# Four PSUM banks in turn, sampled columns on GpSimd, sampled values' products by fours, and other places for the chunks

## The chip, the cores and the metric

The kernel runs on one core of a Trainium2 chip. The metric is the device time of one execution in microseconds; for the kernel before it is the median of three runs. An engine has its own queue of instructions and works it in order: TensorE (PE; its weight loads are PEld), VectorE (DVE), ScalarE (ACT), GpSimd (POOL) and SyncE (SP, which here only issues transfers). Engines wait for each other on semaphores.

## The reference

One decoder step with two mixer branches on the same normalised input: 512 prompt positions and 8 sampled tokens (one each, with states of their own), so 520 columns are carried through all projections.

```python
h = _rmsnorm(x, norm_g)
P = hf @ w_in                                  # one projection for both branches
q, k, v, g_a, sh, g_b, m_a, m_b = split(P)
y_a, s_ret_new = _retention_branch(q, k, v, g_a, pos0, s_ret)      # 4 heads, DK 256, DV 512
y_b, s_rw_new = _rwkv_branch(sh, sh_prev, g_b, ..., s_rw)          # 16 heads of 64
merged = sigmoid(m_a) * (y_a @ w_down_a) + sigmoid(m_b) * (y_b @ w_down_b)
x = x + merged @ w_out
gate = sigmoid(_rmsnorm(x, ple_norm_g) @ w_ple_gate)
x = x + (p @ w_ple) * gate
```

The retention branch is attention with a decay and a state; the RWKV branch is a recurrence `s = s * w - (s kk) (a kk) + v k`, which the kernel solves for the prompt in chunks of 64 positions, two heads at a time. Outputs are the final norm of `x` for prompt and sampled tokens, and all new states.

## The kernel before

**Precision and projections.** Everything is float32. A weight tile `raw` (512 KB) is loaded by SyncE (`fetch`, L136), copied by ScalarE to a rounded `whi` (L141), and VectorE takes the rest as `wlo` (L142). A projection is then three products (`hhi` x `whi`, `hlo` x `whi`, `hhi` x `wlo`, line L154) that accumulate in one PSUM bank, 24 matmuls for one half of the 520 columns. They are the bulk of TensorE's work.

**PSUM.** There are eight banks: pool `ph` has four, for projections (`mm_half`); pool `px` has three, handed out by `bank()`; pool `pq` has one, tag `po`. A bank can be written again when its last reader is done with it.

**Who sets the order.** The functions emit instructions through a scheduler that runs a simulated timeline and places each instruction on its engine's queue by priority and readiness; dependences added by hand (`side_by_side`: order only; `after`: a semaphore) restrict it. Which buffer of a pool a tile gets is settled in the order of the code. So the order on the chip is fixed at build time, and each engine then takes its queue strictly in order.

**Stages in the trace.** To 82 us: input norm, transposes, key projections and the norm sums `pss` (L410). 82 to 262 us: eight RWKV pairs (`pair`, two heads each). 262 to 715 us: four retention heads. 715 to 867 us: the eight RWKV chunks between gate and down projections. To the end: the rest of the down projections, the output projection and the per-layer gates.

**A pair** makes, in this order: two `pn` (L438, norms; read by VectorE into `kkn`), four `pw` (L445 and L446, two products each; read by ScalarE's tanh at L447 into `sg` and `a`), decays and the scaled keys `KRS`, `BK` on VectorE (`km`, L471, on the way); then 16 small products `g` into four banks (L498), which VectorE masks into `GM` (L504); two `pb` (L483, the bonus `bon`); transposes of `BK` (L525) and of the values (L532). `bank()` serves all of these from `px`, but for the fourth bank of `g`, which is `pq`'s. Between the parts stand the next pair's projections `zr`, `zv` (or gates `mg`) as filler. Stores of `KRS`, `GM`, `BKT`, `Vt`, `bon` go to DRAM on SyncE. ScalarE also copies the eight sampled columns of five tensors into `smp` (L488, 40 small copies in all); at the end of the pairs `smp` is transposed (L579), evicted to `sT` (L580) and stored to `SMd` (L581). GpSimd reads `SMd` back as `sv` (L659), prepares constants, and then loads the retention states `tS` (L749), which ScalarE scales (L755).

**A retention head** projects and rotates keys and queries (L792, L801 to L806), then values: `phv` (L827) takes the four weight tiles j = 0 to 3, 24 matmuls each. The sampled tokens' values are made apart, in `vsm` (L822): for j = 1 and 3 four products, each a float32 matmul with 32 columns of the array, one for each of four column groups; a float32 matmul shows as two passes in the trace. `side_by_side` keeps the four in order but lets the scheduler put other work among them, or the next four right behind. In the built program `vsm` stands in groups of 6 and 2 (head 0), 5 and 3 (heads 1 and 3), 5, 2 and 1 (head 2).

**A chunk** (`chunk`) has products `UO` (L1014), `U` (L1023), `dS` (L1029), `UO` again (L1032), with evictions between (`Ot`, L1045). Between the chunks stand 16 fills, eight gates `mg` (L208, stored to `MBd`, L209) and eight down projections `down_a`; the list `AT` says how many fills are emitted up to each chunk. Chunks have a high priority, so the scheduler moves them ahead of fills when they are ready. `loads(c)` (L990 to L999) brings a chunk's `SV`, `KR`, `TT`, `BKt`, `DT`.

Of the kernel before, what the change touches and what calls it, by code (L numbers as in the profile page):

```python
# [8 lines left out]
F32 = mybir.dt.float32  # L9
# [3 lines left out]
ALU = mybir.AluOpType  # L13
# [66 lines left out]
def body(tc, A, O, dbg=None, upto="Z"):  # L80
# [11 lines left out]
    with es:  # L92
# [12 lines left out]
        def ctile(name, shape):  # L105
            return cst.tile(shape, F32, tag=name, name=name)

        def bank(name="x", tag="x"):
            return px.tile([128, 512], F32, tag=tag, name=name)

# [71 lines left out]
        def side_by_side(ms):  # L182

            ms = [getattr(i, "ins", i) for i in ms]
            for x, y in zip(ms, ms[1:]):
                tc.add_manual_dep(y, x.name, mybir.DependencyInfo(mybir.DependencyClass.NoSync, mybir.DependencyReason.SCHED_ONLY),
                                  reason="side by side")

        def after(i, prior):

            tc.add_manual_dep(getattr(i, "ins", i), getattr(prior, "ins", prior).name,
                              mybir.DependencyInfo(mybir.DependencyClass.Sync, mybir.DependencyReason.DATA), reason="together")
# [189 lines left out]
        for p in range(NPAIR):  # L382
# [25 lines left out]
            for j, c0, c1 in HV:  # L408
                for x, w in enumerate(sqs):
                    pe.matmul(pss[j][0:16, 0:c1 - c0], indr[:, p, :], w[:, c0:c1], start=(p == 0 and x == 0), stop=(p == 7 and x == 1))  # L410
        rn2 = pA.tile([32, NT], F32, tag="b1", name="rn")
        rn = rn2[0:16]
# [20 lines left out]
        def pair(p, zr, zv):  # L433
# [44 lines left out]
            def bonus():  # L478
                bon = pA.tile([128, NT], F32, tag="bon", name="bon")
                for j, c0, c1 in HV:  # L480
                    pb = bank("pb")[:, 0:c1 - c0]
                    for x, w in enumerate(rks):
                        pe.matmul(pb, bdr, w[:, c0:c1], start=(x == 0), stop=(x == 1))  # L483
                    dve.tensor_tensor(bon[:, c0:c1], pb, zv[:, c0:c1], ALU.mult)
                act.activation(bon, bon, AF.Identity, bias=vcol(V_LB, p))
                sp.dma_start(BNd[p], bon)
                for i, src, f in ((0, zr, 1.0), (2, km, 1.0), (3, zv, 1.0), (4, kkn, 1.0), (5, b1, 0.5)):
                    act.activation(smp[:, p, i, :], src[:, T:NT], AF.Copy, scale=f)  # L488

            if p == NPAIR - 1:  # L490
# [5 lines left out]
                   else pA.tile([128, NCH, 128], F32, tag=f"W{i}", name="GM", bufs=1) for i in range(2)]  # L496
            gs = [bank("g") for _ in range(3)] + [pq.tile([128, 512], F32, tag="po", name="g")]
            ms = [pe.matmul(gs[2 * q + hh][:, c * 128:(c + 1) * 128], BK[hs_, 4 * q + c, :], KRS[hs_, 4 * q + c, :], start=True, stop=True)  # L498
# [77 lines left out]
        for q in range(2):  # L576
# [3 lines left out]
            act.activation(sT[:, q * 512:(q + 1) * 512], g[0:48], AF.Copy)  # L580
        sp.dma_start(SMd.rearrange("v b d -> (v b) d"), sT)  # L581
        pA_.__exit__(None, None, None)
        for nm, t in dict(KRd=KRd, BKd=BKd, DTd=DTd, XTd=XTd, Vd=Vd, BNd=BNd, SMd=SMd).items():
# [200 lines left out]
        for h in range(H):  # L784
# [33 lines left out]
            for j in range(4):  # L818
                ready = fetch(w_in[256 * j:256 * j + 256, O_V + DV * h:O_V + DV * h + DV])
                raws, w = raws[-1:] + [wide(ready[0])], [wide(t) for t in weights(None, ready=ready)]  # L820
                if j % 2:
                    side_by_side([pe.matmul(vsm[32 * g:32 * g + 32], hst[:, 2 * j - 2 + g, :], raws[g // 2][:, g % 2, :],  # L822
                                            start=(j == 1), stop=(j == 3), skip_group_check=True) for g in range(4)])
                for jt in range(4):
# [263 lines left out]
        nxt_y = beside_rwkv(128, slice(0, 128))  # L1088
        AT = [0, 2, 4, 6, 8, 9, 11, 13, 16]
        for c in range(NCH):  # L1090
# [228 lines left out]
```

## Time and profile before

| what | value |
|---|---|
| time, median of 3 runs | 1083.75 us (1082.77 to 1086.52) |
| profiled execution, its own time | 1085.46 us |
| its span | 1083.3 us |
| mean granted clock of TensorE | 0.992 |
| busy share: PE, DVE, ACT, POOL | 97%, 73%, 46%, 6% |
| data moved | 199.44 MB, 184 GB/s over the span |

The profiled execution is one run with the hardware profiler on; its times of single instructions are what the text argues from. "Busy" is the time in which an engine has at least one instruction in work; matmuls overlap, so a busy TensorE need not be at its peak. A row of the timeline has start, length, engine, line, operation, tiles, and in brackets how long its engine stood before it and what ended that. A row of the waits has the waiting instruction, the one it waited for, the microseconds in all, how often, and the longest.

### The profile page before, as it was taken

Reading aid. Unit: us, or ns where it says so; the run is one execution under the profiler, and the core shown is the slowest. Engines: PE = TensorE matmul, PEld = TensorE weight load, DVE = VectorE, ACT = ScalarE, POOL = GpSimd, SP = SyncE. Lnnn points to the kernel's source line nnn. Section 1 sums busy time; section 2 is a strip of 40 time slices with the busy share of each in tenths; the row PEclk is TensorE's granted clock in tenths of the full one; section 3 lists DMA queues with packets and bytes.
Section 4 is the critical chain, followed back from the end, with each engine's and each line's share of the span. In section 5 each row is a group of like instructions: output and inputs, shape, how many; then the busy total and the mean of one; then the engine's idle time right before and its main releaser. Section 6 shows DMA issues by size and latency. Waiting matters only on the chain.

```text
span 1083.3 us, 22028 instructions
## 1 busy us (share of the span) xinstructions
PE 1049.0 (97%) x8932; PEld 976.5 (90%) x8932; DVE 786.4 (73%) x1429; ACT 500.7 (46%) x1013; POOL 63.1 (6%) x99
## 2 busy tenths in 40 slices
PE   7999999999999999999999999999899999999995
PEld 6999989999979789986989889898898999999995
DVE  6646988784499698959884788855667764656775
ACT  6754655554364644373446234354322224434554
POOL 2000000000300100100020100110001100000000
PEclk9999999999999999999999999999999999999998
DMA  5633588788943933573298643879987558743222
GB/s 179 179 89 87 130 198 201 185 238 228 331 154 108 322 124 99 197 279 97 70 328 208 234 123 108 305 226 319 290 257 222 154 159 241 245 134 92 84 59 80
DMA packets 239223, 199.44 MB, mean 184 GB/s; under 512 B 58988, under 2 KB 203225, under 8 KB 237970
## 3 DMA queue, kind: packets, MB, share of 16 engines
q1 hardware_dynamic: 225586, 149.60, 47.4%
q0 software_dynamic: 13376, 48.17, 12.7%
q8 instruction: 70, 1.15, 0.4%
q14 instruction: 31, 0.25, 0.1%
q10 hardware_dynamic: 160, 0.27, 0.1%
HBM read 137.70 MB, written 60.00 MB: 183 GB/s over the span
## 4 chain that ended last, share of the span: by engine, by line
PE 86%; DMA 7%; DVE 4%; ACT 2%; issue 1%; SPq 0%; DVEq 0%; POOL 0%; POOLq 0%; ACTq 0%
PE ph L154 59%; PE phv L827 8%; PE o L899 3%; PE st L910 2%; DMA raw<-in_w_in_dram 2%; PE sc L852 1%; PE po L761 1%; PE UO L1014 1%; DMA MBd<-mg 1%; PE g L498 1%; DMA yalo<-YAd 1%; PE vsm L822 1%; PE vb L753 1%; DMA tS<-in_state_ret_dram 1%; DMA o<-OSd 1%
## 5 line engine op out<-in xcount | busy, mean ns | idle before, releaser
L154 PE MATMUL ph<-hhi,whi 128*128 128x256 f32 (+2 forms) x1296 | 369.8, 286 | 0.8 <-ACT hhi L275 0.6
L154 PE MATMUL ph<-hhi,wlo 128*128 128x256 f32 (+2 forms) x1296 | 368.7, 285 | 0.5 <-DVE wlo L142 0.5
L154 PE MATMUL ph<-hlo,whi 128*128 128x256 f32 (+2 forms) x1296 | 368.7, 285 | 0.5 <-DVE hlo L276 0.5
L154 PEld LDWEIGHTS ph<-hhi,whi 128*128 128x128 f32 x1296 | 243.5, 188 | 5.0 <-ACT hhi L275 1.0
L154 PEld LDWEIGHTS ph<-hlo,whi 128*128 128x128 f32 x1296 | 243.7, 188 | 3.8 <-DVE hlo L276 1.1
L154 PEld LDWEIGHTS ph<-hhi,wlo 128*128 128x128 f32 x1296 | 244.1, 189 | 1.7 <-DVE wlo L142 0.7
L142 DVE TENSOR_TENSOR wlo<-raw,whi 128x1024 fp32r<-128x1024 f32 x135 | 164.9, 1222 | 102.0 <-ACT whi L141 100.9
L141 ACT ACTIVATE whi<-raw 128x1024 fp32r<-128x1024 f32 x135 | 142.7, 1058 | 207.7 <-PE ph L154 144.2
L154 PE MATMUL ph<-yalo,whi 128*128 128x264 f32 (+1 forms) x256 | 73.2, 287 | 0.0
L154 PE MATMUL ph<-yahi,whi 128*128 128x264 f32 (+1 forms) x256 | 72.6, 285 | 0.0
L154 PE MATMUL ph<-yahi,wlo 128*128 128x256 f32 (+1 forms) x256 | 72.5, 287 | 0.0
L614 DVE TENSOR_TENSOR tm<-M 128x62 f32<-128x62 f32 (+30 forms) x62 | 53.0, 855 | 0.6
L616 DVE TENSOR_TENSOR M<-M,tm 128x62 f32<-128x62 f32 (+30 forms) x62 | 52.9, 853 | 0.5
L827 PE MATMUL phv<-whi,hhi 128*128 128x512 f32 x128 | 51.2, 400 | 0.9 <-ACT whi L141 0.9
L827 PE MATMUL phv<-whi,hlo 128*128 128x512 f32 x128 | 50.5, 395 | 0.0
L154 PEld LDWEIGHTS ph<-yalo,whi 128*128 128x128 f32 x256 | 48.6, 190 | 0.3
L154 PEld LDWEIGHTS ph<-yahi,wlo 128*128 128x128 f32 x256 | 48.4, 190 | 0.3
L154 PEld LDWEIGHTS ph<-yahi,whi 128*128 128x128 f32 x256 | 48.5, 189 | 0.1
L827 PE MATMUL phv<-wlo,hhi 128*128 128x512 f32 x128 | 46.8, 396 | 0.0
L756 DVE SCALAR_TENSOR_TENSOR tS<-vb,ks,tS 128x512 f32<-128x512 f32 x64 | 44.1, 744 | 2.3 <-PE vb L753 2.3
L755 ACT ACTIVATE tS<-tS 128x512 f32<-128x512 f32 x64 | 35.1, 620 | 13.0 <-DMA tS<-in_state_ret_dram 13.0
L154 PE MATMUL ph<-ybhi,whi 128*128 128x264 f32 (+1 forms) x128 | 36.5, 285 | 0.0
(454 smaller groups left out, 2103.0 us busy)
## 6 DMA issues: line engine op xcount, KB each, us to landing
raw<-in_w_in_dram SPq DMA_DIRECT2D x97, 512.0 KB, 3.8
tS<-in_state_ret_dram POOLq DMA_DIRECT2D x16, 1024.0 KB, 8.6
out_dram<-tS POOLq DMA_DIRECT2D x16, 1024.0 KB, 10.1
KR<-KRd SPq DMA_DIRECT2D x8, 1024.0 KB, 9.6
raw<-in_w_down_a_dram SPq DMA_DIRECT2D x16, 512.0 KB, 4.0
KRd<-KRS SPq DMA_DIRECT2D x16, 256.0 KB, 5.1
KRd<-GM SPq DMA_DIRECT2D x16, 256.0 KB
BKt<-BKd SPq DMA_DIRECT2D x8, 512.0 KB, 6.6
```

Source lines behind the costliest of these rows:

```text
L141: cp = act.activation(hi, raw, AF.Copy)
L142: sb = dve.tensor_tensor(lo, raw, hi, ALU.subtract)
L154: m_ = pe.matmul(ps[:, 0:c1 - c0], w[:, k, :], r[:, k0 + k, c0:c1], start=(x == 0), stop=(x == n_ - 1))
L498: ms = [pe.matmul(gs[2 * q + hh][:, c * 128:(c + 1) * 128], BK[hs_, 4 * q + c, :], KRS[hs_, 4 * q + c, :], start=True, stop=True) for q in ...
L614: dve.tensor_tensor(tv, M[:, 0:s, s:s + 1].to_broadcast([128, s, n]), M[:, s:s + 1, s + 1:C].to_broadcast([128, s, n]), ALU.mult)
L616: dve.tensor_tensor(M[:, 0:s, s + 1:C], M[:, 0:s, s + 1:C], tv, ALU.add)
L753: pe.matmul(vb, sel[:, 4 * g + b, :], vsr, start=True, stop=True)
L755: act.activation(S[:, b, :], S[:, b, :], AF.Copy, scale=GAM[h])
L756: last = dve.scalar_tensor_tensor(S[:, b, :], vb, ks[:, h, i, 4 * g + b:4 * g + b + 1], S[:, b, :], ALU.mult, ALU.add)
L827: m_ = pe.matmul(vps[jt], r[:, 2 * j + k, 128 * jt:128 * jt + 128], w_[:, k, :], start=(j == 0 and k == 0 and x == 0), stop=(j == 3 and k ...
L899: pe.matmul(ps, a_[:, o_:o_ + 128], b_[:, jt, :], start=(x == 0), stop=(x == len(seq) - 1))
L910: pe.matmul(ps, a_[:, jt, 128 * i:128 * i + 128], b_[:, jt, :], start=(x == 0), stop=(x == 11))
```

## The change

Four edits. First, `bank()` gets a counter `turn`: from behind the norm sums to the end of the pairs each fourth bank is `pq`'s, so that the pairs rotate through four banks where they had three, and the fourth `g` no longer takes `pq`'s bank by name. Second, the copies into `smp` (but for the one that is an exponential) are made by GpSimd's `tensor_scalar` in place of ScalarE's `activation`. Third, the four `vsm` of a step stay four, and the first of them gets a semaphore wait on `marks[2]`, which is ScalarE's copy `whi` of the same weight tile; `after` is changed to take a raw instruction. Fourth, the list `AT` is another.

```diff
@@ -105,7 +105,13 @@
         def ctile(name, shape):
             return cst.tile(shape, F32, tag=name, name=name)
 
+        turn = [None]
+
         def bank(name="x", tag="x"):
+            if turn[0] is not None:
+                turn[0] = (turn[0] + 1) % 4
+                if turn[0] == 3:
+                    return pq.tile([128, 512], F32, tag="po", name=name)
             return px.tile([128, 512], F32, tag=tag, name=name)
 
         KRd = dr.tile([NCH, 128, 16, 128], F32, tag="KRd", name="KRd")
@@ -188,7 +194,8 @@
 
         def after(i, prior):
 
-            tc.add_manual_dep(getattr(i, "ins", i), getattr(prior, "ins", prior).name,
+            prior = prior if hasattr(prior, "name") else prior.ins
+            tc.add_manual_dep(getattr(i, "ins", i), prior.name,
                               mybir.DependencyInfo(mybir.DependencyClass.Sync, mybir.DependencyReason.DATA), reason="together")
 
         w_in = A["w_in"][0]
@@ -408,6 +415,7 @@
             for j, c0, c1 in HV:
                 for x, w in enumerate(sqs):
                     pe.matmul(pss[j][0:16, 0:c1 - c0], indr[:, p, :], w[:, c0:c1], start=(p == 0 and x == 0), stop=(p == 7 and x == 1))
+        turn[0] = 1
         rn2 = pA.tile([32, NT], F32, tag="b1", name="rn")
         rn = rn2[0:16]
         ssk = pA.tile([16, NT], F32, tag="t1", name="ssk", bufs=1)
@@ -485,7 +493,7 @@
                 act.activation(bon, bon, AF.Identity, bias=vcol(V_LB, p))
                 sp.dma_start(BNd[p], bon)
                 for i, src, f in ((0, zr, 1.0), (2, km, 1.0), (3, zv, 1.0), (4, kkn, 1.0), (5, b1, 0.5)):
-                    act.activation(smp[:, p, i, :], src[:, T:NT], AF.Copy, scale=f)
+                    pool.tensor_scalar(smp[:, p, i, :], src[:, T:NT], f, None, ALU.mult)
 
             if p == NPAIR - 1:
                 bonus()
@@ -494,7 +502,7 @@
 
             GMs = [pA.tile([128, NCH, 128], F32, tag="GM", name="GM") if p < NPAIR - 1
                    else pA.tile([128, NCH, 128], F32, tag=f"W{i}", name="GM", bufs=1) for i in range(2)]
-            gs = [bank("g") for _ in range(3)] + [pq.tile([128, 512], F32, tag="po", name="g")]
+            gs = [bank("g") for _ in range(4)]
             ms = [pe.matmul(gs[2 * q + hh][:, c * 128:(c + 1) * 128], BK[hs_, 4 * q + c, :], KRS[hs_, 4 * q + c, :], start=True, stop=True)
                   for q in range(2) for c in range(4) for hh, hs_ in ((1, hi_), (0, lo_))]
             side_by_side(ms)
@@ -579,6 +587,7 @@
                 pe.transpose(g[0:48, i * 128:(i + 1) * 128], smp[:, 4 * q + i].rearrange("p v b -> p (v b)"), ident)
             act.activation(sT[:, q * 512:(q + 1) * 512], g[0:48], AF.Copy)
         sp.dma_start(SMd.rearrange("v b d -> (v b) d"), sT)
+        turn[0] = None
         pA_.__exit__(None, None, None)
         for nm, t in dict(KRd=KRd, BKd=BKd, DTd=DTd, XTd=XTd, Vd=Vd, BNd=BNd, SMd=SMd).items():
             if nm in dbg:
@@ -819,8 +828,10 @@
                 ready = fetch(w_in[256 * j:256 * j + 256, O_V + DV * h:O_V + DV * h + DV])
                 raws, w = raws[-1:] + [wide(ready[0])], [wide(t) for t in weights(None, ready=ready)]
                 if j % 2:
-                    side_by_side([pe.matmul(vsm[32 * g:32 * g + 32], hst[:, 2 * j - 2 + g, :], raws[g // 2][:, g % 2, :],
-                                            start=(j == 1), stop=(j == 3), skip_group_check=True) for g in range(4)])
+                    ms = [pe.matmul(vsm[32 * g:32 * g + 32], hst[:, 2 * j - 2 + g, :], raws[g // 2][:, g % 2, :],
+                                    start=(j == 1), stop=(j == 3), skip_group_check=True) for g in range(4)]
+                    side_by_side(ms)
+                    after(ms[0], marks[2])
                 for jt in range(4):
                     for k in range(2):
                         for x, (w_, r) in enumerate(((w[0], hhi), (w[0], hlo), (w[1], hhi))):
@@ -1086,7 +1097,7 @@
             loads(1)
         done = []
         nxt_y = beside_rwkv(128, slice(0, 128))
-        AT = [0, 2, 4, 6, 8, 9, 11, 13, 16]
+        AT = [0, 3, 6, 8, 9, 11, 12, 13, 16]
         for c in range(NCH):
             with tc.high_priority(offset=20000):
                 PS = chunk(c)
```

With line numbers of the changed kernel a little higher (L154 is now L160, L445 is L453, L498 is L506, L822 is L831, L827 is L838), the built order changes as follows.

TensorE, the `pw` of the fourth pair, ahead of the third pair's `g`, before (`ph` are the filler's projections, the shape is rows by columns of the result, x16 stands for so many equal rows; `W_466` with `Z_468` and `ZL_470` makes `sg`, `W_467` with `Z_469` and `ZL_471` makes `a`):

```order
L154 MATMUL ph<-hhi,wlo 128x274
L445 MATMUL pw<-Z_468,W_466 128x256
L446 MATMUL pw<-ZL_470,W_466 128x256
L445 MATMUL pw<-Z_468,W_466 128x264
L446 MATMUL pw<-ZL_470,W_466 128x264
L445 MATMUL pw<-Z_469,W_467 128x256
L446 MATMUL pw<-ZL_471,W_467 128x256
L445 MATMUL pw<-Z_469,W_467 128x264
L446 MATMUL pw<-ZL_471,W_467 128x264
L498 MATMUL g<-KRS,BK 128x128 x16
```

and now:

```order
L454 MATMUL pw<-ZL_470,W_466 128x264
L160 MATMUL ph<-hhi,whi 128x274
L160 MATMUL ph<-hlo,whi 128x274
L160 MATMUL ph<-hhi,wlo 128x274
L160 MATMUL ph<-hhi,whi 128x274
L453 MATMUL pw<-Z_469,W_467 128x256
L454 MATMUL pw<-ZL_471,W_467 128x256
L160 MATMUL ph<-hlo,whi 128x274
L160 MATMUL ph<-hhi,wlo 128x274
L453 MATMUL pw<-Z_469,W_467 128x264
L454 MATMUL pw<-ZL_471,W_467 128x264
L506 MATMUL g<-KRS,BK 128x128 x16
```

The four `pw` (each a pair of rows) stood together; now projections stand between them, eight more of them ahead of the piece shown.

TensorE, head 0, the values' step j = 1, before (`phv` are the values' products, `vsm` the sampled ones; the brackets name the semaphores that a row waits for, DMAHW being loads):

```order
L827 MATMUL phv<-wlo,hhi 128x512
L822 MATMUL vsm<-raw,hst 32x512 [waits DMAHW4_49,Pool_49]
L822 MATMUL vsm<-raw,hst 32x512
L822 MATMUL vsm<-raw,hst 32x512 [waits DMAHW6_49]
L822 MATMUL vsm<-raw,hst 32x512
L822 MATMUL vsm<-raw,hst 32x512 [waits DMAHW7_49]
L822 MATMUL vsm<-raw,hst 32x512
L827 MATMUL phv<-whi,hhi 128x512 [waits Activation_49]
L827 MATMUL phv<-whi,hlo 128x512
```

and now:

```order
L838 MATMUL phv<-wlo,hhi 128x512
L831 MATMUL vsm<-raw,hst 32x512 [waits DMAHW4_49,Activation_49,Pool_49]
L831 MATMUL vsm<-raw,hst 32x512
L831 MATMUL vsm<-raw,hst 32x512 [waits DMAHW6_49]
L831 MATMUL vsm<-raw,hst 32x512
L838 MATMUL phv<-whi,hhi 128x512
L838 MATMUL phv<-whi,hlo 128x512
```

The six `vsm` have become four, and the wait for ScalarE has moved from the first `phv` behind them to the first `vsm`.

SyncE, in the chunks, the loads and stores around the first down projections' weights, before (`raw` is a weight tile, `mg` a gate, the others are a chunk's loads):

```order
L136 DMA raw<-in_w_down_a_dram 128x8x128
L995 DMA TT<-TTd 64x1024
L997 DMA BKt<-BKd 128x1024
L209 DMA MBd<-mg 128x520
L990 DMA SV<-Vd 64x512
L991 DMA SV<-Vd 64x512
L999 DMA DT<-DTd 128x512
L136 DMA raw<-in_w_down_a_dram 128x8x128
L993 DMA KR<-KRd 128x2048
```

and now:

```order
L142 DMA raw<-in_w_down_a_dram 128x8x128
L1006 DMA TT<-TTd 64x1024
L1008 DMA BKt<-BKd 128x1024
L142 DMA raw<-in_w_down_a_dram 128x8x128
L1001 DMA SV<-Vd 64x512
L1002 DMA SV<-Vd 64x512
L1010 DMA DT<-DTd 128x512
L216 DMA MBd<-mg 128x520
L1004 DMA KR<-KRd 128x2048
L216 DMA MBd<-mg 128x520
L142 DMA raw<-in_w_down_a_dram 128x8x128
```

One load of a weight tile has moved ahead of three transfers, and the store of one gate behind them.

## The prediction

> **What bounds the kernel now.** I read the page first, then a table of windows over the RWKV pairs, the waits of TensorE there, the timeline around single waits, SyncE's queue, and the chain of work that ended last around the first retention head.
>
> ```profile
> span 1083.3 us, 22028 instructions
> PE 1049.0 (97%) x8932; PEld 976.5 (90%) x8932; DVE 786.4 (73%) x1429; ACT 500.7 (46%) x1013; POOL 63.1 (6%) x99
> PE 86%; DMA 7%; DVE 4%; ACT 2%; issue 1%; SPq 0%; DVEq 0%; POOL 0%; POOLq 0%; ACTq 0%
> ```
>
> TensorE is busy for 97% of the span and has 86% of the last chain. No edit takes a product away, so a gain can only come from the 34 us in which TensorE stands, from matmuls that use part of the array, or from a slow clock. The pairs hold some of that:
>
> ```profile
> 135.00:162.00 27.00, 24.77 (x221) 23.30 (x219) 22.76 (x43) 16.17 (x38) 0.00 (x0) 1.00 0.82 195
> 162.00:189.00 27.00, 26.16 (x226) 25.51 (x227) 23.40 (x42) 13.88 (x29) 0.00 (x0) 1.00 0.82 205
> 189.00:216.00 27.00, 25.96 (x226) 25.49 (x226) 20.55 (x38) 15.88 (x38) 0.00 (x0) 1.00 0.76 183
> 216.00:243.00 27.00, 25.88 (x238) 24.76 (x237) 21.63 (x36) 14.14 (x32) 0.00 (x0) 1.00 0.87 234
> ```
>
> The columns are the length of the window, busy time of PE, PEld, DVE, ACT and POOL, TensorE's clock, the DMA share and GB/s. TensorE stands 2.23 + 0.84 + 1.04 + 1.12 = 5.2 us of these 108 us. VectorE is busy for 88.3 of them and keeps 19.7 us free. The waits view names what it stands for:
>
> ```profile
> PE pw L445 <- ACT sg L447: 2.8, 3, 1.0
> PE g L498 <- ACT a L447: 1.5, 2, 1.0
> PE g L525 <- DVE BK L520: 0.4, 1, 0.4
> PE pb L483 <- DVE GM L504: 0.3, 1, 0.3
> PE g L498 <- ACT sg L447: 0.2, 1, 0.2
> ```
>
> That is 5.2 us again, 4.5 of it for ScalarE's tanh evictions of `pw`. One of them on the timeline (start, length, engine, line):
>
> ```profile
> 155.63 0.28 PE L446 MATMUL pw<-ZL,W 128*128 128x256 f32 x1
> 156.43 0.84 ACT L447 ACTIVATE sg<-pw,hwa 128x256 f32<-128x256 f32 x2
> 156.95 0.19 PEld L445 LDWEIGHTS pw<-Z,W 128*128 128x128 f32 x1 [1.24 <-ACT sg L447]
> ```
>
> Four `pw` come back to back on three banks. The fourth needs the bank of the first, whose eviction started 0.8 us after the third was issued.
>
> **Part 1, the fourth bank and the copies.** With four banks in turn the fourth `pw` needs the bank of the second `pn`, which VectorE reads and which is further back; the first `g` needs the first `pw`. In the order the four `pw` no longer stand together either: 8, 4 and 2 projections lie between them. What remains is `g` behind the last evictions, `T` behind VectorE's `BK`, and `pb` behind `GM`. The copies matter by their place:
>
> ```profile
> L488 ACT ACTIVATE smp<-zr x8: 191/208/210, 85.5 to 195.8; 128x8 f32<-128x8 f32 x8
>   DVE km L471: 6.9, 4
>   DVE kkn L439: 4.5, 5
> 286.97 0.33 POOL L730 MEMSET hst<- 128x256 f32 x1
> 285.62 0.97 POOL L722 MEMSET sel<- 128x1024 f32 x1
> ```
>
> ScalarE loses 40 x 0.2 = 8 us of work and 11.4 us of standing before two kinds of them, with evictions queued behind. On GpSimd I take 0.33 us for one (the smaller memset; up to 0.97), 40 in the 160 us of the pairs, with nothing due sooner behind them there. So I take two thirds of the standing as gone: -3.5 us when TensorE leaves the pairs, with 0 and -5.2 as ends (VectorE at 82% may simply be late next).
>
> This isn't yet the end's gain, since the next stage starts on a transfer chain. SyncE issues the pairs' stores in order, and the last one feeds the sampled state:
>
> ```profile
> 196.25 1.77 SPq L136 DMA_DIRECT2D raw<-in_w_in_dram  x2
> 200.91 0.59 SPq L510 DMA_DIRECT2D KRd<-KRS  x1
> 217.79 0.38 SPq L136 DMA_DIRECT2D raw<-in_w_in_dram  x1
> 218.82 2.68 SPq L510 DMA_DIRECT2D KRd<-KRS  x2
> 276.21 0.38 SPq L581 DMA_DIRECT2D SMd<-sT  x1
> 282.46 4.60 DMA sv<-SMd
> 287.76 8.16 DMA tS<-in_state_ret_dram
> 298.13 0.95 ACT whi L141
> ```
>
> SyncE's last real hole ends at 200.91 (2.89 us) and a small one at 218.82 (0.65 us); from there it issues without pause to 276.21. Then come the landing, `sv`, GpSimd's queue, `tS`, and ScalarE, where the next weights' copy `whi` stands behind `tS`. What TensorE wins before 218 can pull this chain forward, what it wins later cannot. Of the standing, 4.11 us lie before 216; two thirds are 2.7. I take 2.7 us for the chain, with ends 0 (the DMA shares of 0.82 to 0.87 leave little room to issue faster) and 4.1.
>
> **Part 2, the sampled values four at a time.** First head 0, where the wait is added:
>
> ```profile
> 295.94 2.19 ACT L755 ACTIVATE tS<-tS 128x512 f32<-128x512 f32 x4 [4.33 <-DMA tS<-in_state_ret_dram]
> 296.28 1.91 PE L822 MATMUL vsm<-raw,hst 128*32 128x512 f32 x12
> 299.13 0.50 PE L827 MATMUL phv<-whi,hhi 128*128 128x512 f32 x1 [0.94 <-ACT whi L141]
> ```
>
> Today six `vsm` run from 296.28, while ScalarE is still at `tS`, and `phv` goes on at 299.13 after 0.94 us of waiting. With the added wait the four `vsm` start only when `whi` is done (298.13 + 0.95 = 299.08), and every `phv` of this group is queued behind them. ScalarE's order there is unchanged. The other heads show what a group costs:
>
> ```profile
> 394.65 1.90 PE L822 MATMUL vsm<-raw,hst 128*32 128x512 f32 x10
> 396.49 0.50 PE L827 MATMUL phv<-whi,hhi 128*128 128x512 f32 x1
> 405.53 1.06 PE L822 MATMUL vsm<-raw,hst 128*32 128x512 f32 x6
> 406.52 0.50 PE L827 MATMUL phv<-wlo,hhi 128*128 128x512 f32 x1
> ```
>
> Five instructions (ten passes) take 396.49 - 394.65 = 1.84 us, three take 0.99: each uses 32 of 128 columns, four lie side by side, and the fifth starts a second round. A group of four I take at 0.99, by the group of three (ends 0.9 and 1.84, if four don't share the array). Heads 1 and 3 go from 5 + 3 to 4 + 4: -0.85 us each; head 2 from 5 + 2 + 1: -1.84, with the small groups at 0.99. Sum -3.5 us, on TensorE and so on the path; there ScalarE has no `tS` to serve ahead of `whi`, so I price the wait at nothing (up to the 0.94 us of head 0 each if that is wrong).
>
> Head 0 then goes: `whi` done at 299.08 - 2.7 = 296.4, `phv` at 297.4 instead of 299.1: -1.7 us. All that TensorE won beyond this is waited away: it comes at 296.28 - 3.5 = 292.8 and stands 3.6 us. Such standing has a second price:
>
> ```profile
> 764.82 0.97 PE L1014 MATMUL UO<-SV,KR 128*64 128x64 f32 x10 [4.46 <-ACT Ot L1045]
> 764.00:768.00 4.00, 3.18 (x56) 3.18 (x58) 2.62 (x3) 2.21 (x5) 0.00 (x0) 0.58 1.03 322
> 828.26 0.92 PE L1029 MATMUL dS<-SV,BKt 128*64 128x64 f32 x24 [2.31 <-DVE SV L1027]
> 828.00:832.00 4.00, 3.74 (x68) 3.56 (x69) 2.75 (x4) 1.82 (x3) 0.88 (x1) 0.69 1.02 290
> 832.00:836.00 4.00, 4.00 (x48) 3.86 (x49) 3.85 (x9) 1.37 (x2) 0.00 (x0) 0.89 1.04 275
> ```
>
> After a wait of 4.46 us the granted clock is 0.58 over 4 us, a loss of 0.42 x 4 = 1.7 us; after one of 2.31 us it is 0.69 and 0.89, again 1.7 us. Head 0's 3.6 us lie between the two, so I add 1.7 us, with 0 as the other end. Head 0 and the pairs together are then worth 0. By the Trainium skill ("TensorE: Matmul & The Clock Gate", Part 1) the clock drops after an idle window of about 3.4 us in a free-running raster. By that rule 3.6 us of standing would seldom fill a window and cost nothing; the row of 2.31 us speaks against it, and the measurement decides.
>
> **Part 3, the chunks' table.** In the order the chunks' places hardly move: the stall at 764.82 keeps its cause, and one down-projection load goes ahead of a store of `MBd`, whose reader has slack. Before the `dS` at 828.26 stand 41 projections in place of 36. I take -0.5 us: five more at 26.16 / 226 = 0.12 us, by the second window. If the wait falls under what closes the clock, another -1.7; if the moved `MBd` is late, +1 (by the 0.94 us wait above, the nearest).
>
> **The sum**, against the profiled execution's 1085.46 us (span 1083.3, and 2.2 around it): pairs and head 0 -1.7, clock +1.7, heads 1 to 3 -3.5, chunks -0.5: -4.0, so 1081.5. That execution stands 1.7 over the median of 1083.75; the forecast is 1079.8, rounded to 1079.5.
>
> **The rivals.** First, the larger gain: all 5.2 us go, the chain comes 4.1 earlier (`phv` at 295.0 + 1.0 = 296.0, -3.1), the clock stays up at head 0, and the stall at 828 no longer closes it: -3.1 - 3.5 - 0.5 - 1.7 = -8.8, near 1075. For it: the 4.5 us are bank waits of one kind. Against: both clock rows.
>
> Second, no difference: TensorE wins its time in the pairs, but the stores set the next stage, and the chain doesn't move. Then `phv` of head 0 starts at 300.1 (+0.9), the clock costs 1.7, and with -3.5 and -0.5 it is -1.4: 1082.4. For it: SyncE without a pause from 218 on, 0.87 of DMA. Against: the hole of 2.89 us at 200.91.
>
> Third, slower: GpSimd's copies hold VectorE up. Some 28 copies fall into the 108 us of the windows, where VectorE has 19.7 us free. It decides from 0.7 us of VectorE for each; at 0.97 us the pairs end 27.2 - 19.7 = 7.5 us later, the chain with them, and with head 0's +0.9 and +1.7, -3.5 and -0.5 it is +6.1: near 1090. The Trainium skill ("GPSIMD Engine Reference", Specifications) says that GpSimd shares its SBUF interfaces with VectorE; no run here shows such copies. Against: eight columns are little.
>
> That the table does nothing is in the terms, at 0.5 us.
>
> **How the numbers follow.** A measurement of this kernel can tell about 0.3%, 3.25 us: faster is under 1080.5, slower over 1087. The forecast has a chance of 0.45 (1077.5 to 1082 by its terms; some 0.37 of it under 1080.5), the larger gain 0.25, no difference 0.20, slower 0.10. That makes 0.62 faster, 0.28 within, 0.10 slower. The range reaches from 1073.5 (the larger gain, a little more) to 1085 (no difference with the late `MBd` and a group of four dearer than three); it leaves out the third rival.
>
> **What would show it.** Right: in the waits of TensorE over the pairs, `pw` <- `sg` gone and 1 to 2 us left; `vsm` in groups of eight passes at about 1 us; in head 0 a wait of 3 to 4 us before `vsm` and a clock near 0.6 behind it; `SMd`<-`sT` issued about 2.7 us earlier, less than TensorE's lead. Wrong: the old `pw` waits under another name, `SMd` moved by nothing or by all of TensorE's lead, four `vsm` taking 1.84 us, VectorE's instructions longer beside GpSimd's copies.

## The result and the profile after

The changed kernel takes 1076.15 us (median of 11 runs, 1070.04 to 1082.13), the kernel before, run beside it, 1082.77 us (11 runs, 1076.94 to 1086.52): a ratio of 0.994 with a 95% interval of 0.9919 to 0.996. Single runs of either kernel differ by 10 to 12 us, so a single profile weighs little by itself; where the text compares stages, it uses several profiles. Two executions far above the rest (1154 us with the sampled products alone, 2048 us of the changed kernel once more, both below) are left out of the ratios.

The windows over the pairs in the profile after (length, busy PE, PEld, DVE, ACT, POOL, clock, DMA share, GB/s):

```profile
135.00:162.00 27.00, 25.23 (x232) 24.32 (x232) 22.78 (x43) 15.76 (x31) 3.00 (x9) 1.00 0.83 194
162.00:189.00 27.00, 26.27 (x230) 25.81 (x230) 24.99 (x46) 14.71 (x28) 1.77 (x6) 1.00 0.85 219
189.00:216.00 27.00, 27.00 (x243) 26.59 (x243) 22.06 (x40) 15.52 (x32) 4.02 (x8) 1.00 0.79 190
216.00:243.00 27.00, 27.00 (x255) 26.62 (x254) 22.48 (x35) 13.71 (x27) 1.43 (x4) 1.00 0.90 253
```

TensorE now stands 1.77 + 0.73 = 2.5 us of the 108 (5.2 before), none of it in the second half. The waits of TensorE from 80 to 262 us after the change:

```profile
PE g L506 <- ACT a L455: 1.4, 2, 0.7
PE g L506 <- ACT sg L455: 1.1, 1, 1.1
```

All waits before `pw` are gone, and those before the transposes of `BK` and before `pb` too; only the products `g` still wait for the last evictions. TensorE's weight loads, which have waits of their own, stood 7.8 us in the pairs before and 3.1 us now. The place that the prediction showed, on the timeline after:

```profile
153.96 0.28 PE L453 MATMUL pw<-Z,W 128*128 128x256 f32 x1
...
155.21 0.28 PE L453 MATMUL pw<-Z,W 128*128 128x264 f32 x1
...
155.97 0.28 PE L453 MATMUL pw<-Z,W 128*128 128x256 f32 x1
...
156.45 0.28 PE L453 MATMUL pw<-Z,W 128*128 128x264 f32 x1
...
158.62 0.60 PE L506 MATMUL g<-KRS,BK 64*128 64x128 f32 x6 [0.67 <-ACT a L455]
```

The four `pw` are spread over 2.5 us with projections between, and none waits. What is left, 0.67 us, is the last eviction of `a` ahead of the last `g`.

Head 0 after the change, on the timeline of SyncE, ScalarE and TensorE:

```profile
272.56 0.38 SPq L589 DMA_DIRECT2D SMd<-sT  x1
291.71 2.19 ACT L764 ACTIVATE tS<-tS 128x512 f32<-128x512 f32 x4 [3.56 <-DMA tS<-in_state_ret_dram]
293.81 1.04 ACT L147 ACTIVATE whi<-raw 128x1024 fp32r<-128x1024 f32 x1
294.95 1.06 PE L831 MATMUL vsm<-raw,hst 128*32 128x512 f32 x8 [2.64 <-issue]
295.94 0.50 PE L838 MATMUL phv<-whi,hhi 128*128 128x512 f32 x1
```

and two windows there (the clock is the third column from the right):

```profile
292.00:296.00 4.00, 1.36 (x11) 0.24 (x9) 2.04 (x4) 4.00 (x8) 0.00 (x0) 1.00 1.02 399
296.00:300.00 4.00, 4.00 (x21) 3.25 (x18) 3.93 (x9) 4.00 (x10) 0.00 (x0) 1.00 1.02 374
```

TensorE stands 2.64 us before the four `vsm`, which start just after `whi`; the profile puts the wait to "issue", but ScalarE's rows above show what it was. `SMd` leaves 4.3 us earlier than before, once the start is taken off (below). `phv` goes on 0.99 us after the first `vsm`. The clock stays at 1.00 here.

Head 1 after the change:

```profile
391.62 1.06 PE L831 MATMUL vsm<-raw,hst 128*32 128x512 f32 x8
392.61 0.50 PE L838 MATMUL phv<-whi,hhi 128*128 128x512 f32 x1
```

A group of four takes 0.99 us, as three did before.

To compare stages I take where TensorE starts a piece that both kernels have: the first `pss` (the runs start up to 2.4 us apart, which is taken off), the last pair's first `pn`, head 0's first `st`, the first `UO`, the first `so`. These rows of the profile after, whose counterparts before start at 47.09, 230.57, 370.04, 729.34 and 890.38:

```profile
47.70 0.40 PE L417 MATMUL pss<-sqh,indr 128*16 128x256 f32 x2
225.40 0.37 PE L446 MATMUL pn<-rns,inh 128*128 128x256 f32 x1
367.15 0.40 PE L921 MATMUL st<-vhi,dhi 128*128 128x512 f32 x1
722.67 0.51 PE L1025 MATMUL UO<-SV,KR 128*64 128x64 f32 x10
876.42 0.60 PE L1133 MATMUL so<-ident,PS 128*64 128x128 f32 x4
```

So the pairs won 225.40 - 230.57 - 0.61 = -5.8 us, of which +2.3 were lost by the end of head 0; heads 1 to 3 won -3.8, and the chunks -7.3.

The first of these marks needs care. In the new order 20 projections (2.4 us at 0.12 us each) that stood ahead of the last pair's first `pn` stand behind it, so at that mark the lead for equal work is 3.4 us. The transposes of `smp`, at the end of the pairs, have equally many matmuls between them and the first `pss` in both orders; before and after:

```profile
267.97 0.71 PE L579 MATMUL g<-ident,smp 128*48 128x128 f32 x5
263.01 0.71 PE L587 MATMUL g<-ident,smp 128*48 128x128 f32 x5
```

There the lead is 263.01 - 267.97 - 0.61 = -5.6 us, so the pairs' gain is real and 0.2 us less than the table's. The later marks have at most four projections (0.5 us) more or less ahead of them.

The same for all kernels that were run (us against the first profile of the kernel before; each column is one stage):

| kernel | pairs | rest of pairs and head 0 | heads 1 to 3 | chunks |
|---|---|---|---|---|
| table only (same order as before) | 0.0 | -0.7 | 0.0 | -5.7 |
| copies only | 0.0 | +0.4 | 0.0 | -3.3 |
| sampled products only | 0.0 | +1.9 | -3.7 | -7.2 |
| banks only | -5.8 | +1.9 | +1.2 | -4.5 |
| banks and copies | -5.8 | +3.3 | +1.8 | -4.5 |
| whole, without the wait | -5.8 | +3.7 | +2.3 | -4.5 |
| whole change, first profile | -5.8 | +2.3 | -3.8 | -7.3 |
| whole change, second profile | -5.7 | +5.8 | -3.8 | -4.3 |
| whole, old table | -5.7 | +8.6 | -3.8 | -6.1 |
| whole, copies on ScalarE | -5.8 | +4.2 | -3.8 | -8.0 |
| whole, weights' copy first | -5.8 | +2.9 | -3.5 | -5.8 |
| whole, `sv` late | -5.7 | +5.7 | -3.5 | -6.3 |
| whole, both | -5.7 | +6.2 | -3.5 | -5.4 |

The pairs and heads 1 to 3 are the same to a few tenths in each profile of one order. Head 0 and the chunks are not: there TensorE waits for transfers, and in some executions its clock drops behind such a wait.

### The profile page after: what moved, and what is told of

Read it like the earlier page. It is cut to its first block, busy times and chain, and to the rows that moved or that the text cites. A ratio compares the mean times of both kernels' runs of the same rounds, so it can differ in the third digit from the quotient of the medians.

```text
span 1069.7 us, 22049 instructions
## 1 busy us (share of the span) xinstructions
PE 1042.0 (97%) x8932; PEld 974.8 (91%) x8932; DVE 785.2 (73%) x1429; ACT 494.8 (46%) x973; POOL 79.5 (7%) x139
## 4 chain that ended last, share of the span: by engine, by line
PE 85%; DMA 6%; DVE 3%; ACT 2%; issue 1%; SPq 1%; POOL 0%; DVEq 0%; POOLq 0%; ACTq 0%
PE ph L160 58%; PE phv L838 8%; PE o L910 3%; PE st L921 2%; PE sc L863 1%; PE po L770 1%; PE g L506 1%; PE UO L1025 1%; DMA raw<-in_w_ple_gate_dram 1%; DMA raw<-in_w_in_dram 1%; DMA yalo<-YAd 1%; DMA BKt<-BKd 1%; DMA MBd<-mg 1%; PE vb L762 1%; PE vsm L831 1%
## 5 line engine op out<-in xcount | busy, mean ns | idle before, releaser
L160 PE MATMUL ph<-hhi,whi 128*128 128x256 f32 (+2 forms) x1296 | 370.5, 286 | 0.9 <-ACT hhi L282 0.4
L160 PE MATMUL ph<-hlo,whi 128*128 128x256 f32 (+2 forms) x1296 | 369.4, 285 | 0.2 <-DVE hlo L283 0.2
L160 PE MATMUL ph<-hhi,wlo 128*128 128x256 f32 (+2 forms) x1296 | 368.8, 285 | 0.5 <-DVE wlo L148 0.5
L160 PEld LDWEIGHTS ph<-hhi,whi 128*128 128x128 f32 x1296 | 244.2, 189 | 6.1 <-issue 1.7
L160 PEld LDWEIGHTS ph<-hhi,wlo 128*128 128x128 f32 x1296 | 245.0, 189 | 2.2 <-DVE wlo L148 0.7
L160 PEld LDWEIGHTS ph<-hlo,whi 128*128 128x128 f32 x1296 | 244.5, 189 | 1.9 <-DVE hlo L283 0.7
L160 PE MATMUL ph<-yalo,whi 128*128 128x256 f32 (+1 forms) x256 | 72.4, 285 | 0.0
L160 PE MATMUL ph<-yahi,whi 128*128 128x256 f32 (+1 forms) x256 | 72.2, 284 | 0.0
L160 PE MATMUL ph<-yahi,wlo 128*128 128x256 f32 (+1 forms) x256 | 71.9, 285 | 0.0
L838 PE MATMUL phv<-whi,hhi 128*128 128x512 f32 x128 | 51.5, 403 | 0.0
L838 PE MATMUL phv<-whi,hlo 128*128 128x512 f32 x128 | 50.5, 395 | 0.0
L160 PEld LDWEIGHTS ph<-yalo,whi 128*128 128x128 f32 x256 | 48.1, 188 | 0.3
L160 PEld LDWEIGHTS ph<-yahi,whi 128*128 128x128 f32 x256 | 48.1, 188 | 0.2
L160 PEld LDWEIGHTS ph<-yahi,wlo 128*128 128x128 f32 x256 | 47.8, 188 | 0.3
L838 PE MATMUL phv<-wlo,hhi 128*128 128x512 f32 x128 | 46.8, 395 | 0.5 <-DVE wlo L148 0.5
L215 ACT ACTIVATE mg<-ph 128x256 f32<-128x256 f32 (+1 forms) x48 | 17.7, 378 | 41.2 <-PE ph L160 20.6
```

The source lines that it names most:

```text
L160: m_ = pe.matmul(ps[:, 0:c1 - c0], w[:, k, :], r[:, k0 + k, c0:c1], start=(x == 0), stop=(x == n_ - 1))
L215: act.activation(g[:, c0:c1], ps, fn, scale=scale)
L838: m_ = pe.matmul(vps[jt], r[:, 2 * j + k, 128 * jt:128 * jt + 128], w_[:, k, :], start=(j == 0 and k == 0 and x == 0), stop=(j == 3 and k ...
```

## The experiments

Each kernel ran beside the kernel before; a ratio is to that, with its 95% interval.

**Banks alone.**

```diff
+            if turn[0] is not None:
+                turn[0] = (turn[0] + 1) % 4
+                if turn[0] == 3:
+                    return pq.tile([128, 512], F32, tag="po", name=name)
...
-            gs = [bank("g") for _ in range(3)] + [pq.tile([128, 512], F32, tag="po", name="g")]
+            gs = [bank("g") for _ in range(4)]
```

> Only the four banks in turn; copies on ScalarE, sampled products and table as before. If the bank turn removes the waits of the pairs (my theory): the four 'pw' <- 'sg' waits gone, TensorE at head 0's first 'phv' 3 to 5 us earlier than before, the store of SMd 2 to 4 us earlier, and the end 2 to 3.5 us earlier, since head 0 still waits for ScalarE. If the copies on ScalarE were what delayed the evictions (rival): the waits stay, under 'g' <- 'a' or 'pw' <- 'sg', and the end moves by less than 1 us.

Measured: 0.9951 (0.9935 to 0.9968) of the time before. The waits of `pw` are gone, and what is left in the pairs is that of the whole change: `g` 1.4 and 1.1 us. The pairs win 5.8 us. `SMd` leaves at 275.40, which is 3.2 us earlier once the start is taken off. The bank turn is the cause in the pairs. The edit gives a fourth bank and, through the scheduler, the order in which the `pw` are spread; no run separates the two. At the end I expected 2 to 3.5 us; the ratio says 5 us (3.5 to 7.0); the stages of its one profile sum to less (3.1 us, with the chunks against the mean of the four profiles in the order before, -4.1), and one profile cannot settle that.

**Copies alone.**

```diff
-                    act.activation(smp[:, p, i, :], src[:, T:NT], AF.Copy, scale=f)
+                    pool.tensor_scalar(smp[:, p, i, :], src[:, T:NT], f, None, ALU.mult)
```

> Only the 40 sampled copies on GpSimd; three banks as before. My theory (banks first): TensorE's 5.2 us of waits in the pairs fall by 1 us at most, the end by under 1 us. Rival (ScalarE's order was the cause): at least 3 us of the waits go and the end comes 2 us or more earlier. Third rival of the prediction (GpSimd slows VectorE): VectorE's rows in the pairs get longer by 0.1 us or more each beside a copy, and the end comes later.

Measured: 1.0003 (0.9983 to 1.0023). TensorE's waits in the pairs with the copies on GpSimd:

```profile
PE pw L445 <- ACT sg L447: 2.8, 3, 1.0
PE g L498 <- ACT a L447: 1.5, 2, 1.0
PE g L525 <- DVE BK L520: 0.4, 1, 0.4
PE pb L483 <- DVE GM L504: 0.3, 1, 0.3
PE g L498 <- ACT sg L447: 0.2, 1, 0.2
```

They are those of before, row by row: ScalarE's standing before the copies cost nothing. VectorE isn't held up either: the pairs' stage agrees to 0.1 us, and the mean length of each frequent kind of VectorE instruction there to 3 ns.

**Sampled products alone.**

```diff
+                    side_by_side(ms)
+                    after(ms[0], marks[2])
```

> Only the sampled products by fours with the wait. My theory: heads 1 to 3 gain 0.85, 1.84 and 0.85 us, head 0 loses 0.9 us (its 'phv' at 300.1 where it was 299.1) and stands 2.8 us before 'vsm'; in all -2.6 us, or -0.9 if the clock drops after that wait. Rival (a group of four takes two rounds): no gain in heads 1 to 3, the end 1 us later.

Measured: 0.9996 (0.998 to 1.0012). Heads 1 to 3 win 3.7 us (0.9, 2.0 and 0.8). Head 0 loses 1.9, from this row of its timeline:

```profile
299.50 1.06 PE L823 MATMUL vsm<-raw,hst 128*32 128x512 f32 x8 [1.88 <-issue]
```

and this window:

```profile
300.00:304.00 4.00, 4.00 (x17) 2.76 (x10) 3.97 (x8) 4.00 (x9) 0.00 (x0) 0.59 1.03 391
```

After a wait of 1.88 us the clock is 0.59 over 4 us, which costs 1.6 us. My theory with the clock gave -0.9 us, and the interval (-2.2 to +1.3) holds it. It holds the rival's +1 us too; what speaks against the rival is the profile, where each group of four takes 1.0 us and heads 1 to 3 win.

**Table alone.**

```diff
-        AT = [0, 2, 4, 6, 8, 9, 11, 13, 16]
+        AT = [0, 3, 6, 8, 9, 11, 12, 13, 16]
```

> Only the list of the chunks' places. Built, its order on every engine is that of the kernel before but for a handful of rows. My theory now: no difference at all (within 0.2%), and its profile is a second look at the kernel before, whose waits before UO and dS in the chunks show how far these vary from run to run (1 to 5 us each). Rival (the table made the chunk stage faster): 3 us or more earlier.

Measured: 1.0003 (0.9984 to 1.0021). Its waits from 715 to 870 us, in the order of the kernel before:

```profile
PE UO L1014 <- ACT Ot L1045: 3.0, 2, 2.1
PE dS L1029 <- DVE SV L1027: 1.3, 1, 1.3
PE U L1023 <- DVE R L1018: 0.2, 1, 0.2
```

4.5 us, where the first profile of the same order had 5.7 + 2.3 + 1.2 = 9.2 in these rows. About half of the stalls on which the prediction's part 3 was read came with that one execution: the longest stood behind ScalarE's `mg`, which waited 8.4 us there for the store of `MBd`, and 4.8 us here. No effect of the table is shown.

**Banks and copies.** The two edits above together.

> Banks in turn and copies on GpSimd, sampled products and table as before. My theory: as with the banks alone, or up to 1 us better; the rest of the gain of the whole change (2 to 3 us) is missing. Rival (the two need each other: freed ScalarE lets the fourth bank act): 2 us or more better than the banks alone.

Measured: 0.9965 (0.9944 to 0.9986), not better than the banks alone. Nothing shows that the two need each other.

**Whole change without the wait.**

```diff
-                    after(ms[0], marks[2])
```

> The whole change, but the four sampled products don't wait for ScalarE's copy; the four in a row stay a wish of the scheduler's order only. If the wait is what makes groups of four (my theory): groups of 5 and 3 come back, heads 1 to 3 lose up to 3.5 us, head 0 gains 1 us, in all 1 to 2.5 us slower than the whole change. Rival (the wait only costs): 1 us faster.

Measured: 0.9963 (0.9944 to 0.9982), against 0.994 with the wait; the intervals overlap. The groups are again not by four: 6 and 2; 5, 1 and 2; 5, 2 and 1; 5 and 3. Head 1 has a group more than in the kernel before, as with the banks alone, and heads 1 to 3 lose 2.3 us where they win 3.8 with the wait: 6.1 us between the two. So in these heads the wait is worth more beside the banks than alone; at the end the difference is not clear of the intervals.

**Whole change with the old table.** The table's edit is undone.

> The whole change with the old list of the chunks' places. Its order is that of the whole change but for a handful of rows. My theory: the same time as the whole change within 0.2%; its profile is a second look at the changed kernel's chunk stage, with a wait before UO of chunk 2 that may lie anywhere from 1 to 5 us. Rival (the table brought the 7 us that the changed kernel's profile gained in the chunks): 4 us or more slower.

Measured: 0.9936 (0.9911 to 0.9961): the same as the whole. Its profile shows head 0 in an unlucky draw, here on the timeline of ScalarE and TensorE:

```profile
282.26 1.06 ACT L147 ACTIVATE whi<-raw 128x1024 fp32r<-128x1024 f32 x1 [7.82 <-DMA raw<-in_w_in_dram]
288.62 2.13 ACT L735 ACTIVATE sel<-ident 8x1024 fp32r<-8x1024 f32 x2 [4.75 <-POOL sel L731]
291.40 1.04 ACT L147 ACTIVATE whi<-raw 128x1024 fp32r<-128x1024 f32 x1
292.49 0.50 PE L838 MATMUL phv<-whi,hhi 128*128 128x512 f32 x1 [2.09 <-ACT whi L147]
297.58 2.19 ACT L764 ACTIVATE tS<-tS 128x512 f32<-128x512 f32 x4 [3.97 <-DMA tS<-in_state_ret_dram]
300.81 0.64 PE L831 MATMUL vsm<-raw,hst 128*32 128x512 f32 x4 [3.07 <-issue]
```

and with a window behind the last wait:

```profile
300.00:304.00 4.00, 3.19 (x14) 1.92 (x14) 3.26 (x6) 4.00 (x8) 0.00 (x0) 0.74 0.99 354
```

There are three gates in a row (waits that end late and hold up what is queued behind them), not one: a weight tile lands late (282.26), then `sel` waits for GpSimd's memset, which queues behind the landing of `SMd` and holds up the first `whi` of the values (2.09 us of TensorE), then `tS` holds up the second (3.07 us).

**Weights' copy first.** In head 0 the scaling of the first eight state tiles is queued behind the second weights' copy, `whi1` being that copy.

```diff
-                        act.activation(S[:, b, :], S[:, b, :], AF.Copy, scale=GAM[h])
+                        if h == 0 and g == 0:
+                            with tc.issue_after(whi1[0]):
+                                act.activation(S[:, b, :], S[:, b, :], AF.Copy, scale=GAM[h])
+                        else:
+                            act.activation(S[:, b, :], S[:, b, :], AF.Copy, scale=GAM[h])
```

> The whole change, and in head 0 ScalarE scales the first eight state tiles only behind the weights' copy of step j = 1. My theory (head 0 stands behind the transfer of tS through ScalarE's queue): the wait of 2.6 us before the first 'vsm' goes, 'phv' goes on within 1.1 us, the end comes 1.5 to 2.6 us earlier than with the whole change. Rival (the next weight tile itself, or VectorE, is late there): the wait is kept by another cause and the end doesn't move by more than 0.7 us.

Measured: 0.9923 (0.9896 to 0.9951). From its timeline:

```profile
285.48 2.12 ACT L735 ACTIVATE sel<-ident 8x1024 fp32r<-8x1024 f32 x2 [4.41 <-POOL sel L731]
288.26 1.04 ACT L147 ACTIVATE whi<-raw 128x1024 fp32r<-128x1024 f32 x1
290.36 1.05 ACT L147 ACTIVATE whi<-raw 128x1024 fp32r<-128x1024 f32 x1
294.23 0.63 ACT L768 ACTIVATE tS<-tS 128x512 f32<-128x512 f32 x1 [2.81 <-DMA tS<-in_state_ret_dram]
289.35 0.50 PE L846 MATMUL phv<-whi,hhi 128*128 128x512 f32 x1 [1.72 <-ACT whi L147]
```

The second `whi` now runs at 290.36, four microseconds ahead of `tS`, and the wait before `vsm` is gone. The first gate, `sel`, is still there with 1.72 us. This is the lowest ratio of all, but its interval overlaps that of the whole change, and its gain over it (1.4 to 2.4 us by the ratios, against 0.9936 to 0.9945) is not shown.

**`sv` late.** The load of `sv` moves to where the sampled recurrence starts, so that GpSimd no longer waits for `SMd` before it makes `sel` and loads `tS`.

```diff
-        for i in range(6):
-            pool.dma_start(sv[:, i, :], SMd[i].rearrange("b (h k) -> (b h) k", k=C))
...
         def rwkv_sampled():
+            for i in range(6):
+                pool.dma_start(sv[:, i, :], SMd[i].rearrange("b (h k) -> (b h) k", k=C))
```

> The whole change, and GpSimd loads 'sv' from SMd only when the sampled recurrence starts, so that its memset of 'sel' and its loads of 'tS' no longer queue behind the landing of the pairs' last store. My theory (what the pairs win beyond the store chain is lost at head 0, first through 'sel' ahead of the first 'whi' of the values, then through 'tS' ahead of the second): ScalarE's wait of 4 to 5 us before 'sel' goes, TensorE's waits before 'phv' and 'vsm' in head 0 fall from 3 to 6 us in all to under 1 us, and the end comes 2 to 4 us earlier than with the whole change. Rival (the 16 DMA engines are the limit there, at a share of 1.0 from 280 to 300): the earlier 'tS' delays the weight tiles, TensorE stands as long before 'ph' or 'phv', and the end moves by less than 1 us.

Measured: 0.9956 (0.9937 to 0.9975). ScalarE on its timeline:

```profile
270.22 2.11 ACT L735 ACTIVATE sel<-ident 8x1024 fp32r<-8x1024 f32 x2
280.21 1.06 ACT L147 ACTIVATE whi<-raw 128x1024 fp32r<-128x1024 f32 x1 [7.48 <-DMA raw<-in_w_in_dram]
295.13 1.06 ACT L147 ACTIVATE whi<-raw 128x1024 fp32r<-128x1024 f32 x1 [1.57 <-DMA raw<-in_w_in_dram]
```

the longest of TensorE's waits from 262 to 300 us:

```profile
PE vsm L831 <- issue: 3.7, 1, 3.7
```

and a window (the DMA share is the last column but one):

```profile
280.00:286.00 6.00, 4.57 (x36) 4.16 (x35) 4.63 (x7) 3.09 (x6) 2.91 (x6) 1.00 1.04 405
```

`sel` is 13 us earlier than in the first profile of the whole change and waits for nothing, as I expected. But TensorE stands as long, 5.2 us in all from 262 to 300: the weight tiles `raw` now land late, with the DMA engines at a share of 1.04. My theory falls here, and this one profile bears the rival out. The queue behind `SMd` was only one of several waits for transfers.

**Both.** The last two edits together.

> As the one before, and ScalarE also scales the first state tiles only behind the second weights' copy. My theory: like the one before, within 1 us, since 'tS' is then in time. Rival (ScalarE's queue order still blocks): 1 to 2 us better than the one before.

Measured: 0.9949 (0.9926 to 0.9972), within the intervals like the one before, as I expected. TensorE stands 3.5 us for a weights' copy whose tile landed late:

```profile
284.69 0.58 PE L160 MATMUL ph<-hhi,whi 128*128 128x256 f32 x1 [3.50 <-ACT whi L147]
```

**Whole change with the copies on ScalarE.** The copies' edit is undone.

> The whole change with the 40 sampled copies left on ScalarE. My theory, after the copies alone changed nothing: the same time as the whole change within 2 us (0.2%). Rival (with four banks ScalarE is the next limit, and the copies matter): 2 us or more slower, with new waits of TensorE for 'sg' or 'a' in the pairs.

Measured: 0.9955 (0.9934 to 0.9976), beside 0.9945 (0.9924 to 0.9965) of the whole change run beside it: no difference is shown.

**The changed kernel once more.** No edit.

> The changed kernel once more, beside the three above on one chip. My theory: 0.993 to 0.996 of the time before; in its profile 5.6 to 5.9 us won by the last pair's first 'pn' against the same point before, some of it lost again by head 0's second step. Rival (the chunk stage makes the gain): less than 2 us won up to the first UO.

Measured: 0.9945 (0.9924 to 0.9965). The pairs win 5.7 us again, heads 1 to 3 win 3.8, and head 0 has lost all that the pairs won (-5.7 + 5.8). My theory held; the rival's condition, less than 2 us won up to the first `UO`, didn't come: the first `UO` is 3.7 us earlier with the start taken off.

## Why the prediction was right, step by step

The forecast was 1079.5 us with a range of 1073.5 to 1085; measured were 1076.15 and, as a ratio, 0.4 to 0.8% less. The direction and the mechanism hold, the size was short by some 2.5 us: 1076.15 lies below the stretch that I gave to the forecast's own terms (1077.5 to 1082), between it and the larger gain.

- **Bank waits.** Right in mechanism, too small in size. I took two thirds of 5.2 us, 3.5; the pairs won 5.6 to 5.8, more than the upper end, although 2.5 of the 5.2 us are still there. The idle time of a wait is not its whole price: from start to start, all `pw` together took 11.99 us before and 7.92 after, and `pb` 4.56 and 3.87. The windows count a matmul's modelled tail as busy; the waits of the weight loads, 7.8 us before and 3.1 after, are nearer to the gain.
- **Copies.** I laid part of that gain to ScalarE's 11.4 us of standing. That was wrong: alone the copies moved nothing.
- **The store chain.** Right, and it was the step that mattered. TensorE's lead of 5.8 us is not the end's: `tS` starts on ScalarE 293.5 - 295.7 = 2.2 us earlier on the mean (seven profiles of the kernels with the banks and with `sv` where it was, all that don't move the copy, against four without, starts taken off), with single ones from 0.2 later to 4.6 earlier; `SMd` leaves 2.1 us earlier on the same mean. I had 2.7 for both. After head 0 the whole change had won 3.5, 0.0, 1.5 (copies on ScalarE) and lost 2.9 (old table): on the mean 0.5 won. I had 0 for the pairs and head 0 together; that the sum came out so near is in part luck, since single profiles lie 3 us to either side of it. What I had missed is that there are several gates, `sel` and the weight tiles too, and that the next waits for transfers hold TensorE when one gate is opened, as in the profile with `sv` late.
- **The wait in head 0.** Right: between the kernels with the banks, those without the wait come out of head 0 with 2.0 to 3.9 us won (mean 2.8), those with it with 0.5, so it costs some 2.3 us by the means of three and four profiles (those with it reach from 3.5 won to 2.9 lost); alone it cost 1.9. It stood 2.1 to 3.1 us before `vsm`, where I had 3.6. The clock is not as I had it: of the four profiles of the whole change it dropped in head 0 in two (the second one and the old table), each time for 1.7 us as I had priced it; of the profiles shown it stayed at 1.00 after 2.64 us and fell to 0.59 after 1.88. The last section says why.
- **Heads 1 to 3.** -3.5 forecast, -3.8 measured, or -3.5 for equal work (two projections have moved out of this stage), the same in each profile to 0.3. In the time this gain is not shown by itself: the wait in head 0 takes back about half of it, and the intervals of the banks alone (0.9935 to 0.9968) and of the whole change overlap.
- **The table.** Forecast as next to nothing, and no effect measured: undone, it left the time where it was within the interval. That 41 projections stand before `dS` in place of 36 comes from the banks.
- **The chunks.** -0.5 forecast. The means are -4.1 in the four profiles of the order before (0, -5.7, -3.3, -7.2) and -5.7 in the ten of the order with banks, so -1.6; with single ones from 0 to -7.2 and from -4.3 to -8.0 that is not clear of zero, and 0.5 of it is four projections that moved behind this stage. The first profile of before lay at the slow end: TensorE stood 9.2 us in its chunks and the clock dropped twice (3.4 us), while in the three others of its order it stood 4.4 to 6.7 us and the clock dropped once or not at all. In the first profile after it stood 3.6 us with one drop; these two terms together are the -7.3.
- **The sum** from these: 0.5 + 3.8 + up to 1.6, less 0.3 that is lost behind the chunks on the same means, 4.0 to 5.6 us, against 6.6 between the medians and 4.3 to 8.8 by the interval.
- **The rivals.** The first, the larger gain, came in part: the bank waits of `pw` went whole, and in the first profile the chain came more than 4 us earlier and the clock stayed up in head 0, but not every profile repeats this. GpSimd didn't hold up VectorE. The second rival, the transfers that set the next stage, came true in part of the profiles, and the gain of heads 1 to 3 stood all the same.

What stays open: how much of the pairs' gain is the fourth bank and how much the spread order, whether the sampled products win anything in the time beside the banks, and whether the weights' copy ahead of `tS` is worth its 1.4 to 2.4 us.

## What to carry to other kernels

A burst on a rotating set of buffers is paid in waits of the first eviction; one more buffer in the turn removed them here, together with the spread order that the scheduler then made. A lead won in one stage counts only as far as the transfers that open the next stage move with it, so follow these before you book the gain; when one gate in front of busy transfers is taken away, the next one can hold the same line, as with `sv` late. Before you compare two orders at a mark, count the work ahead of it. And take more than one profile of a stage that waits for transfers before you cost anything from its stalls.

## What was not expected of the hardware

GpSimd's copies of 8 columns take 0.23 us, but some take up to 1.48. One such copy and VectorE's instruction beside it, in the profile of the whole change:

```profile
141.88 1.09 POOL L496 TENSOR_SCALAR smp<-b 128x8 f32<-128x8 f32 x1 [0.60 <-DVE b L474]
...
141.71 1.23 DVE L458 TENSOR_TENSOR_SCAN cum<-reset,sg 128x520 f32<-128x520 f32 x1
```

The copy ends at 142.97, with the end of the scan (142.94), which reads two tensors from SBUF. Of the 40 copies, the eleven of more than 0.5 us all ran beside an instruction of VectorE with such operands; those beside one that reads PSUM took 0.23 (a few that touched a two-input instruction did, too). In ten of the eleven VectorE's instruction had started first (here at 141.71, against 141.88). So here it was GpSimd that waited, and the edit alone cost VectorE nothing that the pairs' stage shows. The Trainium skill ("GPSIMD Engine Reference", Specifications) names contention with VectorE's instructions with two SBUF inputs, and the trace agrees.

The clock: 0.59 over 4 us after TensorE stood 1.88 us, and 1.00 after 2.64 us. The length of the wait alone doesn't decide; where it falls does. In the fourteen profiles the granted clock is recorded as 1.0 or 0.5 and changes only on a raster of 3.41 us that runs through the whole execution. Here are windows laid on that raster, two of the sampled products alone and one of the whole change (length, busy PE, PEld, DVE, ACT, POOL, clock, DMA share, GB/s):

```profile
297.27:300.68 3.41, 1.53 (x11) 0.37 (x10) 2.23 (x5) 3.41 (x8) 0.00 (x0) 1.00 1.02 394
300.68:304.10 3.42, 3.42 (x9) 2.68 (x9) 3.39 (x7) 3.42 (x8) 0.00 (x0) 0.50 1.03 388
290.64:294.05 3.41, 1.67 (x8) 1.00 (x6) 2.18 (x6) 2.34 (x5) 0.00 (x0) 1.00 1.01 401
```

In the first TensorE stands 3.41 - 1.53 = 1.88 us, and the next window has half the clock. The 2.64 us of the whole change are split by the raster: 1.74 us fall into the third row's window and 0.90 into the next, and the clock stays at 1.00. From 30 to 1055 us of the fourteen profiles, all 21 windows at full clock in which TensorE stood 1.8 us or more were followed by half the clock; four with 1.74 to 1.79 us were not, and of those below that only one was (1.66 us). One such drop costs half of 3.41 us, 1.7 us. The Trainium skill ("TensorE: Matmul & The Clock Gate", Part 1) has a free-running window, by which the moment would matter too, and the traces agree; its 3.4 us as the least idle time is not what the first row shows.
